# One fourth-degree polynomial in place of two refinement steps in every norm's inverse root, and the first half's mean taken ahead

## The chip, the cores and the metric

The kernel runs on one core of a Trainium2 chip. Its time is the device time of one execution in microseconds (us), as the median of three executions. The core has five engines with a queue of instructions each: TensorE (PE in the profile, its weight loads PEld), VectorE (DVE), ScalarE (ACT), GpSimd (POOL) and SyncE (SP), which issues most of the transfers. An engine takes its instructions strictly in the order of its queue, and waits on semaphores where data or buffers come from another engine.

## The reference

Two layers of an encoder trunk over 512 tokens of width 1024, in float32. Layer 0 mixes the tokens with a bidirectional gated recurrence (HGRN2, 8 heads), layer 1 with latent attention (MLA, 16 heads). Both then have the same MLP and a gated per-layer embedding, and everything is wrapped in RMS norms.

```
def rms_norm(x, gain):
    xf = x.astype(jnp.float32)
    y = xf * lax.rsqrt(jnp.mean(xf * xf, axis=-1, keepdims=True) + EPS)
    return (y * gain.astype(jnp.float32)).astype(x.dtype)

    for i in range(DEPTH):
        a = rms_norm(h, pre_mix_norm[i])
        ...                                   # m = hgrn2_mixer(a, ...) or mla_mixer(a, ...)
        h = h + rms_norm(m, post_mix_norm[i])
        f = squared_relu_mlp(rms_norm(h, pre_mlp_norm[i]), w_mlp_in[i], w_mlp_out[i])
        h = h + rms_norm(f, post_mlp_norm[i])
        e = p[i].astype(h.dtype) @ w_ple_proj[i]
        g = jax.nn.sigmoid(h @ w_ple_gate[i])
        h = h + rms_norm(g * e, ple_norm[i])
```

Inside the mixers, `hgrn2_mixer` norms every head's output, and `mla_mixer` norms the compressed query (width 384) and the compressed key and value (width 256). Only the `lax.rsqrt` of such norms is touched here.

## The kernel before

Every matrix product is made of three float32r passes over a high and a low part of both operands: for a weight, DMA brings `raw`, ACT casts it to `whi`, and DVE (at some places POOL) subtracts to get `wlo`; for activations the pairs are `ah`/`al`, `oh`/`ol`, `cqh`/`cql`, `Kh`/`Kl` and so on. A group of matmuls therefore waits for ACT and then for DVE. The products land in PSUM banks (`mm`, `sm`, `nm`), and a bank can be written again only when its reader, mostly an ACT or DVE instruction, is done.

A norm works on tokens as partitions: column t of a small tile belongs to token tile t (128 tokens). ACT squares a tile and sums along the row (`junk`, with the sum in `ssq`; one column for the first 512 elements of the row, one for the second). `Rms.mean` adds the two (`ssq`), scales and adds the epsilon (`sv`); `rsqrt` makes the inverse root (`sr`); then DVE updates the residual (`H<-F,sr,H`, called H below). `Rms.done` calls `mean` and `rsqrt`; `Rms.about` calls `mean` and only `guess`, a first approximation, for norms whose scale is put right later. `Norm.rs` uses `rsqrt` in the two norms of MLA (`nv` to `nr`, four columns), and `scan()` in each HGRN head (`oss` to `orr`, four columns). In the chains between the stages two token tiles go at a time (two columns); the last norm of the program takes one tile at a time (one column).

Before the change `rsqrt` is a shift and a multiply-add on the integer bits (`rq_i`, then `sr`), two scaled copies of the mean square (`rq_m`, `rq_n`), and two refinements: `rq_t` = y y m, then a product that sharpens it, then `sr`; and once more `rq_t` = y y m2 and `sr`. Each instruction but the two copies needs the one ahead of it.

What sets the order: a scheduler simulates the whole program and writes each engine's queue. Instructions issued through `V` it may move; in the stretches between the stages the program asks for program order on PE and on the norms' small operations (`VN`), among which it may still mix others. So the number and length of a few small instructions decide where casts, splits and residual updates stand around them. All go through one helper, so nearly every row of the profile shows line 147 (split helpers show 112), and rows are told apart by tile names.

The stretches of the prediction: the HGRN heads (50 to 305 us, the last head's recurrence about 260 to 305); the way from the layer-0 mixer to its MLP (about 335 to 355); the turn between the layers (about 735 to 760), where the gate's output gets its norm, H is updated and normed again (`r`), and PE transposes it for MLA's input product; MLA's start (780 to 813); and the end (from 1523).

Of the kernel before, what the change touches and what calls it, by code (L numbers as in the profile page):

```python
# [22 lines left out]
F32 = mybir.dt.float32  # L23
F32R = mybir.dt.float32r
I32 = mybir.dt.int32
AF = mybir.ActivationFunctionType
ALU = mybir.AluOpType
AX = mybir.AxisListType.X

P = 128  # L30
S = 512
D = 1024
NB = D // P
NT = S // P
# [127 lines left out]
def trunk(  # L162
# [7 lines left out]
    VN = Ordered(tc, nc.vector, V.mem)  # L170
# [7 lines left out]
    def T(pool, shape, tag, bufs=1, dt=F32):  # L178
        uid[0] += 1
        return pool.tile(list(shape), dt, tag=tag, bufs=bufs, name=f"{tag}_{uid[0]}")  # L180

    cst = ctx.enter_context(tc.tile_pool(name="cst", bufs=1))
# [189 lines left out]
    def linear_outer(keys, xs, pss=None, ws=None, ks=None):  # L372
# [6 lines left out]
                mm3(ps, cols(wh, n, P)[:, k], cols(wl, n, P)[:, k], xs[k][0], xs[k][1], k == 0, k == n - 1)  # L379
        return pss  # L380

    def rsqrt(v, y):


        n = v.shape[1]
        new = lambda tag, dt=F32: T(cst, [P, NT], tag, dt=dt, bufs=2)[:, :n]
        i, m, m2, t = new("rq_i", I32), new("rq_m"), new("rq_n"), new("rq_t")
        VN.tensor_scalar(i, v.bitcast(I32), 1, None, op0=ALU.logical_shift_right)
        VN.tensor_scalar(y.bitcast(I32), i, -1, 0x5F3759DF, op0=ALU.mult, op1=ALU.add)
        VN.tensor_scalar(m, v, 0.375 ** 0.5, None, op0=ALU.mult)  # L390
        VN.tensor_scalar(m2, v, -0.5, None, op0=ALU.mult)

        def times_squared(m):
            if n > 2:
                VN.tensor_mul(t, y, y)
                VN.tensor_mul(t, t, m)
            else:
                for c in range(n):
                    cs = slice(c, c + 1)
                    VN.scalar_tensor_tensor(t[:, cs], y[:, cs], m[:, cs], y[:, cs], op0=ALU.mult, op1=ALU.mult)  # L400


        times_squared(m)
        VN.scalar_tensor_tensor(t, t, -1.25 / 0.375 ** 0.5, t, op0=ALU.add, op1=ALU.mult)
        VN.scalar_tensor_tensor(y, t, 1.875, y, op0=ALU.add, op1=ALU.mult)
        times_squared(m2)
        VN.scalar_tensor_tensor(y, t, 1.5, y, op0=ALU.add, op1=ALU.mult)

    class Norm:

# [253 lines left out]
    for n in range(2):  # L664
        t = T(hp, [P, S], f"am{n}")
# [210 lines left out]
    for k in range(8):  # L876
        step({0: 2, 1: 2, 3: 1, 4: 1, 6: 1}.get(k, 0))
        if k < 7:
            if k % 2 == 0:
                w = W.next(("wo", 0, 0, 0, k // 2))  # L880
# [7 lines left out]
    half_of = lambda n: slice(n * S, n * S + S)  # L888
    espill = nc.dram_tensor("e_spill", (2, NT, P, D), F32).ap()

    def guess(v, y):

        i = T(cst, [P, NT], "gs_i", dt=I32, bufs=2)[:, : v.shape[1]]
        VN.tensor_scalar(i, v.bitcast(I32), 1, None, op0=ALU.logical_shift_right)
        VN.tensor_scalar(y.bitcast(I32), i, -1, 0x5F3759DF, op0=ALU.mult, op1=ALU.add)

    class Rms:


# [8 lines left out]
        def mean(self, ts):  # L908
            sl = slice(ts[0], ts[-1] + 1)
            v, u, w = self.v[:, sl], self.s[:, 0, sl], self.s[:, 1, sl]  # L910
            if self.halves:
                VN.tensor_add(u, u, w)
            if self.eps is None:
                VN.tensor_scalar(v, u, 1.0 / D, EPS, op0=ALU.mult, op1=ALU.add)
            else:
                VN.scalar_tensor_tensor(v, u, 1.0 / D, self.eps[:, sl], op0=ALU.mult, op1=ALU.add)
            return v, self.r[:, sl]

        def done(self, ts):
            rsqrt(*self.mean(ts))  # L920
            return self.r

        def about(self, ts):


            guess(*self.mean(ts))
            return self.r
# [339 lines left out]
    n, gate = mlp_to_gate(0, *mlp(0, act, pss, eps))  # L1267
# [91 lines left out]
    for k in range(2):  # L1359
        c = T(mp, [P, S], "P", 6)  # L1360
# [122 lines left out]
    for k in range(7):  # L1483
        if k % 2 == 0:
            w = W.next(("wo", 1, 1, 0, k // 2))
# [11 lines left out]
    n, gate = mlp_to_gate(1, *mlp(1, act, pss, eps))  # L1497


    for t in range(NT):  # L1500
        u = gate(t, V=VN, apart=True)
        r = n.done((t,))
        for c in range(2):
            cs = half_of(c)
# [56 lines left out]
```

## Time and profile before

| | before |
|---|---|
| median of 3 executions | 1533.91 us (1533.54 to 1535.32) |
| the profiled execution | 1534.51 us, its span 1532.8 us |
| PE busy | 1500.9 us, 98% of the span |
| DVE, ACT, POOL busy | 66%, 50%, 12% |
| mean granted TensorE clock | 0.996 of full |

Start with PE: it is busy nearly all the time, so the time can only shrink where PE waits, where its clock is low, or ahead of its first and behind its last matmul. The list of PE's waits says on which tile; the timeline of a wait then shows which instruction stood ahead in the releasing engine's queue. About 32 us of the span are not covered by PE, in many pieces that are mostly under 2 us.

### The profile page before, as it was taken

To read this page: it belongs to the slowest core of one execution; us is meant where nothing else is said; L and a number is where in the kernel's file an instruction comes from. 1 tells how busy PE (TensorE), PEld (TensorE's weight loads), DVE (VectorE), ACT (ScalarE), POOL (GpSimd) and SP (SyncE) were. 2 spreads that over 40 slices of the span, in tenths; PEclk is the share of its full clock that TensorE was granted. 3 is DMA by queue.
4 is the path that set the end of the run, shared out by engine and by line. 5 is a ranking of instruction groups with operands and counts; after the bars stand their busy time and mean duration, and the time that the engine had idled before them with its cause. 6 is when DMAs were issued, how large, how long until landed. Compare 5 with 4: busy or idle time off the path is not lost.

```text
span 1532.8 us, 19321 instructions
## 1 busy us (share of the span) xinstructions
PE 1500.9 (98%) x7403; PEld 1256.2 (82%) x7403; DVE 1013.1 (66%) x1816; ACT 772.8 (50%) x1327; POOL 191.1 (12%) x208
## 2 busy tenths in 40 slices
PE   9999999999999999999999999999999999999997
PEld 7888888889888787888887888888788887878886
DVE  5788568655575849456787784378464747677476
ACT  6655455256554454434645564466355645444332
POOL 5242132200000000000113331432000000000000
PEclk9999999999999999999999999999999999999999
DMA  6622332147050422323321111221452050604221
GB/s 190 184 83 56 83 83 84 41 128 255 29 192 28 152 68 83 110 70 123 119 88 30 42 56 52 63 75 37 174 197 83 26 194 1 220 1 137 73 92 55
DMA packets 110014, 147.86 MB, mean 96 GB/s; under 512 B 4845, under 2 KB 78178, under 8 KB 109666
## 3 DMA queue, kind: packets, MB, share of 16 engines
q1 hardware_dynamic: 109346, 145.58, 29.1%
q8 instruction: 58, 0.95, 0.3%
q10 hardware_dynamic: 576, 1.05, 0.2%
q14 instruction: 34, 0.28, 0.1%
HBM read 138.23 MB, written 8.39 MB: 96 GB/s over the span
## 4 chain that ended last, share of the span: by engine, by line
PE 88%; DVE 8%; ACT 3%; issue 1%; DMA 0%; POOL 0%; SPq 0%; DVEq 0%; ACTq 0%; POOLq 0%
PE mm L147 81%; PE sm L147 5%; DVE wlo L147 2%; PE nm L147 1%; DVE rope_d L147 1%; ACT whi L147 1%; DVE ol L147 1%; DVE r L268 1%; DVE F L147 1%; ACT junk L147 1%; DMA x<-in_x 0%; DVE al L147 0%; DVE rq_t L147 0%; DVE mx L147 0%; DVE rope_a L147 0%
## 5 line engine op out<-in xcount | busy, mean ns | idle before, releaser
L147 PE MATMUL mm<-ah,whi 128*128 128x512 f32 (+1 forms) x912 | 332.7, 370 | 2.3 <-ACT whi L147 1.0
L147 PE MATMUL mm<-ah,wlo 128*128 128x512 f32 (+1 forms) x912 | 329.6, 368 | 0.0
L147 PE MATMUL mm<-al,whi 128*128 128x512 f32 (+1 forms) x912 | 318.2, 368 | 0.0
L147 ACT CAST whi<-raw 128x1024 fp32r<-128x1024 f32 (+3 forms) x195 | 197.0, 1017 | 218.3 <-PE mm L147 184.2
L147 DVE TENSOR_TENSOR wlo<-raw,whi 128x1024 fp32r<-128x1024 f32 x165 | 207.4, 1266 | 141.3 <-ACT whi L147 139.7
L147 PEld LDWEIGHTS mm<-ah,whi 128*128 128x128 f32 x912 | 172.0, 189 | 31.5 <-ACT whi L147 2.6
L147 PEld LDWEIGHTS mm<-ah,wlo 128*128 128x128 f32 x912 | 172.0, 189 | 27.6
L147 PEld LDWEIGHTS mm<-al,whi 128*128 128x128 f32 x912 | 164.3, 189 | 27.1
L147 PE MATMUL mm<-wlo,oh 128*128 128x512 f32 x400 | 156.3, 391 | 4.0 <-DVE wlo L147 4.0
L147 DVE TENSOR_TENSOR wlo<-r,whi 128x1024 fp32r<-128x1024 f32 x84 | 102.0, 1221 | 80.9 <-ACT whi L147 80.9
L147 PE MATMUL mm<-whi,ol 128*128 128x512 f32 x400 | 154.8, 389 | 0.0
L147 PE MATMUL mm<-whi,oh 128*128 128x512 f32 x400 | 151.6, 392 | 0.7 <-DVE F L147 0.7
L147 ACT CAST whi<-r 128x1024 fp32r<-128x1024 f32 x84 | 87.3, 1051 | 90.9 <-PE mm L147 90.8
L147 PE MATMUL mm<-whi,al 128*128 128x512 f32 x304 | 119.1, 392 | 0.8 <-DVE al L147 0.8
L147 PE MATMUL mm<-whi,ah 128*128 128x512 f32 x304 | 119.3, 394 | 0.2 <-ACT ah L147 0.2
L147 PE MATMUL mm<-wlo,ah 128*128 128x512 f32 x304 | 118.7, 390 | 0.0
L112 POOL TENSOR_TENSOR wlo<-raw,whi 128x512 fp32r<-128x512 f32 (+2 forms) x40 | 38.2, 979 | 560.0 <-ACT whi L147 553.0
L147 PEld LDWEIGHTS mm<-wlo,oh 128*128 128x128 f32 x400 | 75.3, 188 | 21.0 <-DVE wlo L147 5.7
L147 PEld LDWEIGHTS mm<-whi,oh 128*128 128x128 f32 x400 | 75.2, 188 | 16.5 <-DVE F L147 1.1
L147 PEld LDWEIGHTS mm<-whi,ol 128*128 128x128 f32 x400 | 75.2, 188 | 15.6
L147 ACT CAST oh<-Z 128x512 fp32r<-128x512 f32 x84 | 51.5, 620 | 43.6 <-PE mm L147 42.6
L147 PEld LDWEIGHTS mm<-whi,al 128*128 128x128 f32 x304 | 57.1, 188 | 14.2 <-DVE al L147 2.5
(314 smaller groups left out, 2706.9 us busy)
## 6 DMA issues: line engine op xcount, KB each, us to landing
raw<-in_w_mlp_in SPq DMA_DIRECT2D x32, 1024.0 KB, 5.7
r<-in_w_mlp_out SPq DMA_DIRECT2D x24, 1024.0 KB, 8.6
raw<-in_hg_w_in SPq DMA_DIRECT2D x40, 512.0 KB, 5.3
raw<-in_w_mlp_out SPq DMA_DIRECT2D x8, 1024.0 KB, 5.0
raw<-in_w_ple_gate SPq DMA_DIRECT2D x8, 1024.0 KB, 5.7
raw<-in_mla_w_o SPq DMA_DIRECT2D x8, 1024.0 KB, 5.1
raw<-in_mla_w_uq SPq DMA_DIRECT2D x8, 576.0 KB, 4.0
raw<-in_hg_w_out SPq DMA_DIRECT2D x4, 1024.0 KB, 5.1
```

The costliest lines, as they stand in the source:

```text
L112: lo_eng.tensor_sub(dst(lo)[:, a], src(t)[:, a], f(dst(hi))[:, a])
L147: i = getattr(self.eng, name)(*args, **kw)
L268: nc.vector.tensor_sub(quad(t, *u), quad(t, *u), quad(t, *v))
```

## The change

`rsqrt` now takes the guess in one instruction (the integer bits, read as numbers, times -0.5 plus a constant), scales the mean square once (`rq_m`), forms z = y y m (`rq_z`), two quadratics in z that need only z (`rq_p`, `rq_q`), multiplies the first by y, and the two together. `guess`, used by `about` too, shrinks from two instructions to one. `mean` no longer adds the two half sums first: the first half's scaled sum with the epsilon is taken by one instruction that needs only the first column, and the second half is multiplied and added by another (`sv<-ssq,sv`).

```
     def rsqrt(v, y):
         n = v.shape[1]
-        VN.tensor_scalar(i, v.bitcast(I32), 1, None, op0=ALU.logical_shift_right)
-        VN.tensor_scalar(y.bitcast(I32), i, -1, 0x5F3759DF, op0=ALU.mult, op1=ALU.add)
-        VN.tensor_scalar(m, v, 0.375 ** 0.5, None, op0=ALU.mult)
-        VN.tensor_scalar(m2, v, -0.5, None, op0=ALU.mult)
...
-        times_squared(m)
-        VN.scalar_tensor_tensor(t, t, -1.25 / 0.375 ** 0.5, t, op0=ALU.add, op1=ALU.mult)
-        VN.scalar_tensor_tensor(y, t, 1.875, y, op0=ALU.add, op1=ALU.mult)
-        times_squared(m2)
-        VN.scalar_tensor_tensor(y, t, 1.5, y, op0=ALU.add, op1=ALU.mult)
+        guess(v, y)      # y bits = -0.5 * (v bits) + 0x5F3759DF, one tensor_scalar
+        VN.tensor_scalar(m, v, 0.7235449657159028, None, op0=ALU.mult)
...                       # z = y*y*m: two tensor_mul if n > 2, else one instruction per column
+        VN.scalar_tensor_tensor(p, z, -0.65371664, z, op0=ALU.add, op1=ALU.mult)
+        VN.scalar_tensor_tensor(q, z, -3.06928481, z, op0=ALU.add, op1=ALU.mult)
+        VN.scalar_tensor_tensor(p, p, 0.89352604, y, op0=ALU.add, op1=ALU.mult)
+        VN.scalar_tensor_tensor(y, q, 2.75651422, p, op0=ALU.add, op1=ALU.mult)
...
     def mean(self, ts):
-            if self.halves:
-                VN.tensor_add(u, u, w)
             if self.eps is None:
                 VN.tensor_scalar(v, u, 1.0 / D, EPS, op0=ALU.mult, op1=ALU.add)
...
+            if self.halves:
+                VN.scalar_tensor_tensor(v, w, 1.0 / D, v, op0=ALU.mult, op1=ALU.add)
```

VectorE's queue has 1592 rows where it had 1662; the other queues have the same instructions, some in another order. On VectorE, in the turn between the layers, the second norm (`sr_5545`, after it `sr_5511`) stands among the splits `al` of the first two token tiles. Before:

```order
L147 TENSOR_SCALAR sr_5545<-rq_i_6334 128x2
L147 TENSOR_SCALAR rq_m_6335<-sv_5544 128x2
L147 TENSOR_SCALAR rq_n_6336<-sv_5544 128x2
L147 SCALAR_TENSOR_TENSOR al_738_6076<-mm_6323,gains_82,ah_737_6075 128x256
L147 SCALAR_TENSOR_TENSOR rq_t_6337<-sr_5545,rq_m_6335 128x1 x2
L147 SCALAR_TENSOR_TENSOR rq_t_6337<-rq_t_6337 128x2
L147 SCALAR_TENSOR_TENSOR sr_5545<-rq_t_6337,sr_5545 128x2
L147 SCALAR_TENSOR_TENSOR rq_t_6337<-sr_5545,rq_n_6336 128x1 x2
L147 SCALAR_TENSOR_TENSOR sr_5545<-rq_t_6337,sr_5545 128x2
L147 SCALAR_TENSOR_TENSOR H_493<-F_2948,sr_5545,H_493 128x1024 x2
```

and after:

```order
L147 TENSOR_SCALAR sr_5511<-sv_5510 128x2
L147 TENSOR_SCALAR rq_m_6288<-sv_5510 128x2
L147 SCALAR_TENSOR_TENSOR al_730_6030<-sm_6250,gains_82,ah_729_6029 128x256
L147 SCALAR_TENSOR_TENSOR rq_z_6289<-sr_5511,rq_m_6288 128x1 x2
L147 SCALAR_TENSOR_TENSOR al_732_6032<-sm_6259,gains_82,ah_731_6031 128x256
L147 SCALAR_TENSOR_TENSOR al_734_6034<-mm_6268,gains_82,ah_733_6033 128x256
L147 SCALAR_TENSOR_TENSOR rq_p_6290<-rq_z_6289 128x2
L147 SCALAR_TENSOR_TENSOR rq_q_6291<-rq_z_6289 128x2
L147 SCALAR_TENSOR_TENSOR rq_p_6290<-rq_p_6290,sr_5511 128x2
L147 SCALAR_TENSOR_TENSOR sr_5511<-rq_q_6291,rq_p_6290 128x2
L147 SCALAR_TENSOR_TENSOR H_493<-F_2924,sr_5511,H_493 128x1024 x2
L147 SCALAR_TENSOR_TENSOR al_736_6036<-mm_6277,gains_82,ah_735_6035 128x256
```

The last of the eight `al` now stands behind H, the earlier ones further up, and fewer instructions depend on each other behind the seventh. On ACT in the same place, one of the weight casts that stood ahead of the first two `r<-H,sr` stands behind them, and the last `ah` of the eight behind the second pair of `Z<-mm`.

On VectorE at the start of MLA, the norm of the compressed key and value (`nr_6666`, after it `nr_6614`) ends among a weight split and the other norm's squares (`nacc`). Before:

```order
L147 SCALAR_TENSOR_TENSOR nr_6666<-rq_t_6729,nr_6666 128x4
L147 TENSOR_TENSOR rq_t_6729<-nr_6666 128x4
L112 TENSOR_TENSOR wlo_6847<-raw_6682,whi_6846 128x384
L147 TENSOR_TENSOR rq_t_6729<-rq_t_6729,rq_n_6728 128x4
L147 TENSOR_TENSOR nacc_6662<-nacc_6662,nsq_6815 128x512
L147 SCALAR_TENSOR_TENSOR nr_6666<-rq_t_6729,nr_6666 128x4
L147 SCALAR_TENSOR_TENSOR cql_829_6819<-mm_6766,gains_82,cqh_828_6818 128x512
L147 TENSOR_REDUCE nv_6664<-sm_6822 128x4
```

and after:

```order
L147 SCALAR_TENSOR_TENSOR rq_p_6676<-rq_p_6676,nr_6614 128x4
L147 SCALAR_TENSOR_TENSOR nr_6614<-rq_q_6677,rq_p_6676 128x4
L112 TENSOR_TENSOR wlo_6789<-raw_6630,whi_6788 128x384
L147 TENSOR_TENSOR nacc_6610<-nacc_6610,nsq_6760 128x512
L147 SCALAR_TENSOR_TENSOR cql_827_6764<-mm_6711,gains_82,cqh_826_6763 128x512
L147 SCALAR_TENSOR_TENSOR P_6737<-mm_6347,gains_82,rope_a_6688 128x512
L147 SCALAR_TENSOR_TENSOR P_6743<-mm_6348,gains_82,rope_a_6688 128x512
L147 TENSOR_REDUCE nv_6612<-sm_6767 128x4
```

The norm is complete ahead of the split and of `nacc`; PE's transposes of `nr` stand one matmul further up, ahead of those of `nacc`; and the two `P`, which need `nr`, stand ahead of the other norm's sum (`nv`), whose chain is spread over what follows.

On VectorE on the way from the layer-0 mixer to its MLP, the fourth weight split of the MLP's first group (`wlo_3283`, after it `wlo_3249`) stands near the second H update. Before:

```order
L147 SCALAR_TENSOR_TENSOR rq_t_3247<-rq_t_3247 128x2
L112 TENSOR_TENSOR wlo_3283<-raw_3163,whi_3282 128x1024
L147 SCALAR_TENSOR_TENSOR sr_2967<-rq_t_3247,sr_2967 128x2
L147 SCALAR_TENSOR_TENSOR al_429_2972<-sm_3206,gains_82,ah_428_2971 128x256
L147 SCALAR_TENSOR_TENSOR al_431_2974<-sm_3215,gains_82,ah_430_2973 128x256
L147 SCALAR_TENSOR_TENSOR al_433_2976<-mm_3224,gains_82,ah_432_2975 128x256
L147 SCALAR_TENSOR_TENSOR rq_t_3247<-sr_2967,rq_n_3246 128x1 x2
L147 SCALAR_TENSOR_TENSOR al_435_2978<-mm_3233,gains_82,ah_434_2977 128x256
L147 SCALAR_TENSOR_TENSOR sr_2967<-rq_t_3247,sr_2967 128x2
L147 SCALAR_TENSOR_TENSOR H_493<-F_2948,sr_2967,H_493 128x1024 x2
```

and after:

```order
L147 SCALAR_TENSOR_TENSOR rq_p_3217<-rq_p_3217,sr_2943 128x2
L147 SCALAR_TENSOR_TENSOR al_431_2950<-sm_3186,gains_82,ah_430_2949 128x256
L147 SCALAR_TENSOR_TENSOR al_433_2952<-mm_3195,gains_82,ah_432_2951 128x256
L147 SCALAR_TENSOR_TENSOR sr_2943<-rq_q_3218,rq_p_3217 128x2
L147 SCALAR_TENSOR_TENSOR H_493<-F_2924,sr_2943,H_493 128x1024 x2
L112 TENSOR_TENSOR wlo_3249<-raw_3134,whi_3248 128x1024
L147 SCALAR_TENSOR_TENSOR al_435_2954<-mm_3204,gains_82,ah_434_2953 128x256
```

The split and the last `al` went behind the two H. On ACT one of the last `e<-mm` went behind the first `junk<-H`.

In the HGRN heads PE's groups of a head's recurrence (`osq`, `D,E`, `v,As`) stand one to nine matmuls further up; in the last head, after the `am` copy that stood ahead of a `wlo` (272.54 us in the trace before), VectorE now takes `E<-E,oml,L` first, then the `e` copies, and the `wlo` behind those, and POOL takes `As` ahead of the two `D`. Near the layer-1 mixer's end some casts changed places with norms' instructions on ACT; the order of the MLPs' long stretches is as it was but for single `junk`.

## Rows read from the trace of the kernel before

**Rows 1.** The page's summary: span; busy us, share, instructions of an engine.
```profile
span 1532.8 us, 19321 instructions
PE 1500.9 (98%) x7403; PEld 1256.2 (82%) x7403; DVE 1013.1 (66%) x1816; ACT 772.8 (50%) x1327; POOL 191.1 (12%) x208
```

**Rows 2.** PE's waits: tile waited for, us in total, times, longest.
```profile
PE mm L147 <- ACT P L147: 2.2, 2, 1.9
...
PE sm L147 <- ACT r L147: 2.0, 3, 0.7
```

**Rows 3.** Timeline of the end, DVE: start, duration, instruction [idle before].
```profile
1526.02 0.16 DVE L147 TENSOR_TENSOR ssq<-ssq 128x1 f32<-128x1 f32 x1
1526.21 0.15 DVE L147 TENSOR_SCALAR sv<-ssq 128x1 f32<-128x1 f32 x1
...
1526.59 0.15 DVE L147 TENSOR_SCALAR sr<-rq_i 128x1 int32<-128x1 int32 x1
1526.66 0.14 DVE L147 TENSOR_SCALAR rq_m<-sv 128x1 f32<-128x1 f32 x1
...
1526.84 0.22 DVE L147 SCALAR_TENSOR_TENSOR rq_t<-sr,rq_m 128x1 f32<-128x1 f32 x1
1527.09 0.16 DVE L147 SCALAR_TENSOR_TENSOR rq_t<-rq_t 128x1 f32<-128x1 f32 x1
...
1527.93 0.75 DVE L147 SCALAR_TENSOR_TENSOR H<-F,sr,H 128x512 f32<-128x512 f32 x1
```

**Rows 4.** Timeline of the turn between the layers, PE and ACT.
```profile
737.98 1.04 ACT L147 CAST whi<-raw 128x1024 fp32r<-128x1024 f32 x1
738.92 2.19 ACT L147 ACTIVATE r<-H,sr 128x1024 f32<-128x1024 f32 x2
...
741.16 0.98 PE L147 MATMUL sm<-ident,r 128*128 128x128 f32 x7 [0.71 <-ACT r L147]
746.67 0.39 PE L147 MATMUL mm<-ah,whi 128*128 128x256 f32 x1 [0.44 <-DVE rq_n L147]
758.80 0.87 PE L147 MATMUL sm<-ident,r 128*128 128x128 f32 x6 [0.71 <-ACT r L147]
```

**Rows 5.** Timeline of the turn, the second norm on DVE and POOL beside it.
```profile
747.20 2.82 POOL L112 TENSOR_TENSOR wlo<-raw,whi 128x256 fp32r<-128x256 f32 x4 [445.42 <-ACT whi L147]
747.33 0.63 DVE L147 SCALAR_TENSOR_TENSOR rq_t<-rq_t 128x2 f32<-128x2 f32 x1
750.27 2.48 DVE L147 SCALAR_TENSOR_TENSOR H<-F,sr,H 128x1024 f32<-128x1024 f32 x2
```

**Rows 6.** Two windows: us, PE, PEld, DVE, ACT, POOL busy, granted clock, DMA share, GB/s.
```profile
281.80:285.20 3.40, 3.40 (x17) 3.30 (x16) 1.25 (x3) 1.01 (x8) 0.00 (x0) 0.50 0.00 0
800.60:804.10 3.50, 3.50 (x10) 2.71 (x9) 3.37 (x8) 1.23 (x2) 0.00 (x0) 0.51 0.51 169
```

**Rows 7.** Timeline of MLA's start, DVE and PE.
```profile
785.92 0.16 DVE L147 SCALAR_TENSOR_TENSOR nr<-rq_t,nr 128x4 f32<-128x4 f32 x1
787.92 1.40 DVE L147 SCALAR_TENSOR_TENSOR P<-mm,gains,rope_a 128x512 f32<-128x512 f32 x2
798.60 0.47 PE L147 MATMUL mm<-Kh,Qh 128*128 128x512 f32 x1 [1.07 <-ACT whi L147]
800.04 0.51 PE L147 MATMUL mm<-Kl,Qh 128*128 128x512 f32 x1 [0.97 <-DVE Kl L147]
```

**Rows 8.** Timeline of the last HGRN head, DVE and PE.
```profile
276.50 1.87 DVE L147 SCALAR_TENSOR_TENSOR E<-E,oml,L 128x512 f32<-128x512 f32 x1
279.85 0.55 PE L147 MATMUL nm<-ident,ke 128*128 128x128 f32 x3 [1.62 <-DVE state L147]
```

**Rows 9.** Timeline from the layer-0 mixer to its MLP, DVE and PE.
```profile
346.06 1.23 DVE L112 TENSOR_TENSOR wlo<-raw,whi 128x1024 fp32r<-128x1024 f32 x1
349.29 2.48 DVE L147 SCALAR_TENSOR_TENSOR H<-F,sr,H 128x1024 f32<-128x1024 f32 x2
350.18 0.28 PE L147 MATMUL mm<-ah,whi 128*128 128x256 f32 x1
```

More of the change, by code (lines that the diff above doesn't have):

```diff
@@ L380, in linear_outer, with guess @@
         return pss
+    def guess(v, y):
+        VN.tensor_scalar(y.bitcast(I32), v.bitcast(I32), -0.5, float(0x5F3759DF), op0=ALU.mult, op1=ALU.add)
     def rsqrt(v, y):
         n = v.shape[1]
-        new = lambda tag, dt=F32: T(cst, [P, NT], tag, dt=dt, bufs=2)[:, :n]
-        i, m, m2, t = new("rq_i", I32), new("rq_m"), new("rq_n"), new("rq_t")
-        VN.tensor_scalar(i, v.bitcast(I32), 1, None, op0=ALU.logical_shift_right)
-        VN.tensor_scalar(y.bitcast(I32), i, -1, 0x5F3759DF, op0=ALU.mult, op1=ALU.add)
-        VN.tensor_scalar(m, v, 0.375 ** 0.5, None, op0=ALU.mult)
-        VN.tensor_scalar(m2, v, -0.5, None, op0=ALU.mult)
[L393 to L400, printed above, removed]
-        times_squared(m)
-        VN.scalar_tensor_tensor(t, t, -1.25 / 0.375 ** 0.5, t, op0=ALU.add, op1=ALU.mult)
-        VN.scalar_tensor_tensor(y, t, 1.875, y, op0=ALU.add, op1=ALU.mult)
-        times_squared(m2)
-        VN.scalar_tensor_tensor(y, t, 1.5, y, op0=ALU.add, op1=ALU.mult)
+        m, z, p, q = (T(cst, [P, NT], tag, bufs=2)[:, :n] for tag in ("rq_m", "rq_z", "rq_p", "rq_q"))
+        guess(v, y)
+        VN.tensor_scalar(m, v, 0.7235449657159028, None, op0=ALU.mult)
+        if n > 2:
+            VN.tensor_mul(z, y, y)
+            VN.tensor_mul(z, z, m)
+        else:
+            for c in range(n):
+                cs = slice(c, c + 1)
+                VN.scalar_tensor_tensor(z[:, cs], y[:, cs], m[:, cs], y[:, cs], op0=ALU.mult, op1=ALU.mult)
+        VN.scalar_tensor_tensor(p, z, -0.65371664, z, op0=ALU.add, op1=ALU.mult)
+        VN.scalar_tensor_tensor(q, z, -3.06928481, z, op0=ALU.add, op1=ALU.mult)
+        VN.scalar_tensor_tensor(p, p, 0.89352604, y, op0=ALU.add, op1=ALU.mult)
+        VN.scalar_tensor_tensor(y, q, 2.75651422, p, op0=ALU.add, op1=ALU.mult)
     class Norm:
@@ L889, in trunk @@
     espill = nc.dram_tensor("e_spill", (2, NT, P, D), F32).ap()
[L891 to L895, printed above, removed]
     class Rms:
```

## The prediction

> **What bounds the kernel now.** I read the summary first: PE is busy 1500.9 us of a span of 1532.8 [rows 1], so at most 32 us can be had in all by anything that leaves the matmuls as they are, and PE's instructions are the same 6866 rows of its queue before and after. Then PE's waits, by the tile waited for [rows 2]: the list is short, the longest single wait of those shown is 1.9 us, and the small tiles of a norm hardly appear in it. The reader is to see that a shorter norm is not itself a time saved: it counts where the norm's result is what PE waits for, or where it lets a cast, a split or a residual update behind it start earlier. So I went through PE's waits in the timeline and asked of each which queue released it and what stands ahead there now. Last I read the granted clock in windows: it is at full speed but for two stretches at half speed, one in the last HGRN head and one at MLA's start, both behind waits of PE [rows 6].
>
> The profiled execution took 1534.51 us: its span and 1.7 us around it. That is 0.60 above the median of 1533.91. I sum against 1534.51 and take 0.60 off.
>
> **The end of the program.** Nothing covers the last norm, since PE has finished; the path is ssq, then the small instructions, then H and the last transfer. From the start of ssq at 1526.02 to the start of H at 1527.93 are 1.91 us [rows 3]. The starts tell two prices: an instruction that needs the one ahead of it starts 0.19 to 0.25 later (ssq to sv 0.19, rq_t to rq_t 0.25), one that doesn't starts 0.07 later (sr to rq_m). Now: the first half's sv is out of the way before; sv of the second half, guess 0.19 later, rq_m 0.07 beside it, rq_z 0.22 after the guess, rq_p 0.25 later, rq_q beside it, the product with y 0.20 after rq_p, the last product 0.20, H 0.20: 0.19 + 0.22 + 0.25 + 0.20 + 0.20 + 0.20 = 1.26. Gain 0.65. Two prices are not in the trace: the guess as one float operation on integer bits, and sv as an instruction with a third operand. From below they are the 0.15 of the tensor_scalar and from above the 0.22 of the slowest three-operand row [rows 3], so the gain lies between 0.5 and 0.75. I take **-0.63**.
>
> **The turn between the layers.** Three things.
> (a) PE's transposes of the first two tiles of r wait for r, the second time 0.71 with the resumption at 741.16; the three waits for r in this turn sum to 2.0 [rows 2, 4], so the first of this pair is about 0.6. ACT reaches r at 738.92, behind a cast of 1.04 whose start is 0.94 ahead of it [rows 4]. That cast now stands behind both r. The residual that r needs is done before, as ACT goes from the cast to r without a wait. So r comes 0.94 earlier, and PE, which needs both r before it can go on, resumes 0.9 earlier: -0.9. The cast's own product is the last of the four outputs of PE's next product, which starts several us later, so it has cover.
> (b) At 746.67 PE waits 0.44 [rows 4]. The record names rq_n, but PE reads nothing of it here; what frees its bank is the second Z<-mm on ACT. One ah now stands behind it instead of ahead: -0.4. What that ah feeds is the last of eight blocks of PE's product, which has as much cover.
> (c) At 758.80 PE waits 0.71 for r of the second pair [rows 4]. Its chain starts at H, 750.27 [rows 5]. One al and three dependent small instructions no longer stand ahead of H; and the refinement ran into POOL's four wlo from 747.20 on, where a product that takes 0.16 at the end of the program took 0.63 [rows 3, 5]. The chain now ends around 747.5 to 748, H starts some 2 us earlier, and the second norm behind it saves another 0.6: even with PE itself 1.3 earlier the wait goes, -0.7.
> Together **-2.0**. The cap is the sum of the waits, 2.0 + 0.44, with some refilling of PE around them: -3.0; the least is 0, if ACT loses at another cast what it gains here.
>
> A rule of the Trainium skill speaks against (c). The row shows the 0.63 product beside POOL's wlo [rows 5]. "SBUF — State Buffer", section "Who interferes with whom", says that a DVE instruction with two inputs in SBUF contends with a GpSimd instruction that reads SBUF, and that whichever issues later is blocked until the other is done. The row agrees: 0.63 is about one of the four POOL instructions. All four products of the new polynomial have two such inputs, so by the rule, if the chain is not through by 747.20, it is held for up to 4 x 0.47 = 1.9 us, H gains next to nothing, and the sum would lose the 0.7 of (c).
>
> **The start of MLA.** nr of the key and value norm is done at 785.92 + 0.16, behind a wlo and the nacc addition; P, which needs it, starts at 787.92 [rows 7]. Now both come behind nr, and three dependent instructions, 0.2 each [rows 3], are gone: nr is done some 1.5 us earlier. PE's transposes of nr move up by only one matmul, so P starts about 1 us earlier, and the other norm's chain, as much shorter, is spread over splits. PE waits 1.07 and 0.97 further down [rows 7]; the first ends when DVE frees the bank (rope_a<-mm,COS), the second with Kl, and both stand in this same DVE queue, which runs almost without a pause there (3.37 of 3.50 us in the window behind) [rows 6]. If DVE is 0.4 to 1.3 earlier there, so is PE: -1.0. The half-clock stretch behind it [rows 6] costs half of its 3.5 us, less what PE then waits for the next operand (stk): 1.4. I do not count on it going, and add -0.4 for the chance. **-1.4**, between -0.3 (only the small instructions' own time) and -3.5 (both waits and the stretch).
>
> **The last HGRN head.** PE waits 1.62 for state, and runs at half clock for 3.4 us a little later [rows 6, 8], which costs 1.7. The cause stands in DVE's queue: E takes 1.87 at 276.50 beside POOL, where instructions of the same size take 0.75 [rows 3, 8], and ke, which must precede state, waits for E and for the e copies behind a wlo. Now E and the e copies stand ahead of that wlo. The same work remains, so ke may be 1 to 2 us earlier or as late as now, if the contention with POOL falls elsewhere. **-0.9**, between +1.0 and -4.0. In the earlier heads PE hardly waits, and other matmuls stand between a head's norm and its transposes; no term.
>
> **From the layer-0 mixer to its MLP.** This is a loss. PE runs here without a wait and reaches the fourth group of the MLP's first block at 350.18 [rows 9]. The wlo that this group needs was at 346.06; it now stands behind both H. H starts at 349.29 now; the wlo (1.23) goes from ahead of it, an al too (256 columns, which I put at 0.45, between the 0.75 of 512 columns and the 0.16 of a small instruction [rows 3]), and some 0.3 of small instructions: H at 347.3. The two H take 2.48, the wlo 1.23: done at 351.0, against PE's need of the low part one matmul after 350.18, at about 350.3. **+0.65**, between 0 and +1.4. The e that went behind the first junk<-H is ready before that.
>
> **Elsewhere.** In layer 1's way to the MLP one wait on ACT may shrink by a cast's place; the gates lose a tenth here or there: 0, between -0.5 and +0.4. The MLPs are as they were.
>
> Sum: -0.63 - 2.0 - 1.4 - 0.9 + 0.65 = -4.3. 1534.51 - 4.3 - 0.60 = 1529.6; I forecast **1529.7 us**.
>
> **The rivals.**
> *The waits pass to others.* The tail's -0.63 and the cast's -0.9 at the turn are had, and the rest of PE's waits keep their length, since ACT or POOL release them a little later in their own order; layer 0 adds 0.65. -0.9: 1533.0, no change. For it: most of PE's waits are named for ACT or a bank, not for a norm. Against: at the turn the same queue order that shortens the norm moves the cast.
> *The clock stays up.* Both half-clock stretches follow waits that may now be shorter. If PE's waits ahead of them shrink to under 1 us, 1.7 and 1.4 come back on top, less the 0.4 counted: 1527.0. For it: both stretches come after waits of 1 to 1.6 us, which the change shortens [rows 7, 8]. Against: the longest wait of all, 1.9 for P [rows 2], has no such stretch behind it, so length alone doesn't tell.
> *Slower: the split behind H.* In layer 0 the wlo behind both H starts only when H does. If H starts as late as before (349.29), because the ah of ACT that its queue neighbours need come no earlier, the wlo ends at 353.0 and PE waits 2.7; a wait of that size may be followed by a half-clock stretch, 1.7 more. With the same delay the chains behind H lose what the turn gains: +4.4 - 0.6 gives 1537.7. It decides once H starts later than about 348.5, where PE's wait grows past the 1.62 that stands ahead of the half-clock stretch in the last head [rows 8]. Against it: ACT's order there has one cast fewer ahead of those ah.
>
> **How the numbers follow.** A change of 0.2%, 3.07 us, is about what can be told from none here; the bounds are 1530.84 and 1536.98. The forecast 0.50, its own range 1527.8 to 1531.5, with a tenth of all chance above 1530.84; the waits that pass on 0.28; the clock 0.12; the split 0.10, of which 0.08 beyond 1536.98. So faster 0.40 + 0.12 = 0.52, plus 0.03 of the second case; same 0.10 + 0.25 + 0.02 = 0.37; slower 0.08. The range for 8 in 10 runs from 1526.6, which holds nearly all of the clock's case, to 1533.8, above the second.
>
> **What would show it.** Right: H starts about 1.3 us behind ssq at the end; at the turn ACT goes to r without the cast and PE's two waits are one of under half a us, with none at the second r; P starts before PE's nacc product is reduced; PE shows a new wait of half a us for a wlo near 350. Wrong: PE's gaps at the turn and at MLA's start are as long as before with another releaser, or a stretch at half clock where there was none.

## The result, and the profile after

The changed kernel takes 1549.46 us (median of 4 executions, 1547.11 to 1549.87) where the one before, run beside it, takes 1534.49: a ratio of 1.0094 [1.0082, 1.0105]. The forecast was 1529.7 us; the change made the kernel 15 us slower. The page of the profiled execution (1549.87 us), against [rows 1]:

```profile
span 1548.1 us, 19250 instructions
PE 1515.2 (98%) x7403; PEld 1259.5 (81%) x7403; DVE 1000.0 (65%) x1738; ACT 771.9 (50%) x1327; POOL 191.4 (12%) x208
```

DVE has 13 us less to do, as the shorter polynomial says, and PE has the same 7403 instructions. But PE is busy 14.3 us longer. Waits are not the bulk of it then: the matmuls themselves take longer, or run at half clock.

To find where, I took the start of one and the same matmul (by its operands and its number among its kind) in the trace before and in another trace. The difference says how late the other kernel is at that point; the difference between two such points is what the stage between them lost (us; times are those of the kernel before; e1, e2 and e5 are experiments told below). Each column is one profiled execution, and the columns add up to the differences of the spans.

| stage, up to | forecast | after | e1: after, tiles back in place | e2: before, tiles shifted | e5: e1, order mended |
|---|---|---|---|---|---|
| first HGRN heads, 262.9 | 0 | +0.91 | +0.36 | +0.05 | +0.23 |
| last head and output product, 338.6 | -0.9 | +1.63 | -1.87 | -0.49 | -1.90 |
| way to layer 0's MLP, 363.7 | +0.65 | +0.48 | +0.83 | +0.26 | +0.43 |
| **layer 0's MLP and gate, 726.5** | 0 | **+4.11** | -0.01 | **+4.28** | +0.04 |
| turn between the layers, 767.3 | -2.0 | -1.16 | -1.20 | +0.02 | -1.18 |
| MLA's start, 826.9 | -1.4 | +1.02 | +1.94 | +0.06 | +0.81 |
| rest of MLA, 1128.4 | 0 | +0.06 | -0.10 | +0.07 | -0.50 |
| **way to layer 1's MLP, 1158.0** | 0 | **+4.75** | **+3.46** | +0.01 | -0.27 |
| **layer 1's MLP and gate, 1518.0** | 0 | **+4.07** | -0.03 | **+4.28** | 0.00 |
| the end | -0.63 | -0.52 | -0.28 | +0.17 | -0.51 |
| sum | -4.3 | +15.3 | +3.1 | +8.7 | -2.9 |

Three stages make 12.9 of the 15.3 us, and the forecast had 0 in each. How far can one execution be trusted? In the six experiments that keep the order of before (e2, e3, e8 to e11), the way to layer 1's MLP differs from before by 0.01 at most, and in the nine whose weights stand to `oh` and `ol` as before each MLP differs by 0.12 at most. The last head and MLA's start are less steady: in those six they come out between -1.5 and 0 and between +0.1 and +1.6, mostly by stretches at half clock that come and go (last section).

**The MLPs: a slower beat.** In the MLP PE hardly waits, in either kernel. Its timeline in a product of the MLP, first of the kernel before (start, duration, instruction):

```profile
519.94 0.39 PE L147 MATMUL mm<-whi,oh 128*128 128x512 f32 x1
520.17 0.39 PE L147 MATMUL mm<-wlo,oh 128*128 128x512 f32 x1
520.40 0.39 PE L147 MATMUL mm<-whi,ol 128*128 128x512 f32 x1
```

and the same kind of product in the kernel after, and some 50 us ahead of it another kind:

```profile
470.03 0.39 PE L147 MATMUL mm<-ah,wlo 128*128 128x512 f32 x1
470.26 0.39 PE L147 MATMUL mm<-ah,whi 128*128 128x512 f32 x1
470.49 0.39 PE L147 MATMUL mm<-al,whi 128*128 128x512 f32 x1
...
519.92 0.40 PE L147 MATMUL mm<-whi,ol 128*128 128x512 f32 x1
520.15 0.39 PE L147 MATMUL mm<-whi,oh 128*128 128x512 f32 x1
520.39 0.40 PE L147 MATMUL mm<-wlo,oh 128*128 128x512 f32 x1
```

The column to read is the first, not the second: matmuls overlap, so the duration hides the beat. `oh` and `ol` products start every 0.227 us before and every 0.233 after, while `ah` products keep 0.227 to the row. Over all 512-column matmuls the median from start to start goes from 227 ns to 233 or 234 for the 1200 with `oh` or `ol`, and to 232 to 235 for the 408 with `r` or `Z`; for the some 3100 whose operands are `ah` or `al` with `whi` or `wlo` it stays at 227 in both. 1608 times 6 ns are 9.6 us.

**The way to layer 1's MLP: a new wait and half clock behind it.** The timeline after, ACT, DVE and PE, and then a window (columns as in [rows 6]):

```profile
1144.14 1.05 ACT L147 CAST whi<-raw 128x1024 fp32r<-128x1024 f32 x1 [0.32 <-DMA raw<-in_w_mlp_in]
1144.20 2.48 DVE L147 SCALAR_TENSOR_TENSOR H<-F,sr,H 128x1024 f32<-128x1024 f32 x2
1145.10 0.83 ACT L147 ACTIVATE ah<-mm,gains 128x256 fp32r<-128x256 f32 x2
1146.59 0.87 DVE L147 SCALAR_TENSOR_TENSOR al<-mm,gains,ah 128x256 fp32r<-128x256 f32 x2
1147.22 0.55 PE L147 MATMUL mm<-ah,whi 128*128 128x256 f32 x1 [2.84 <-DVE al L147]
```

```profile
1147.00:1151.00 4.00, 3.78 (x18) 3.81 (x19) 2.34 (x8) 3.34 (x4) 0.00 (x0) 0.50 0.41 151
```

PE waits 2.84 us for a bank that the last two `al` read. They stand behind both H on DVE, since the shorter norm lets H go first, and the `ah` they need stand behind a weight cast on ACT. PE idled before the window and gets half its clock in it. In the kernel before, all `al` stood ahead of H and PE waited 0.94 here, for something else:

```profile
1137.55 0.38 PE L147 MATMUL mm<-ah,whi 128*128 128x256 f32 x1 [0.94 <-ACT e L147]
1138.84 0.48 DVE L147 SCALAR_TENSOR_TENSOR al<-mm,gains,ah 128x256 fp32r<-128x256 f32 x1 [0.15 <-ACT ah L147]
1139.24 2.47 DVE L147 SCALAR_TENSOR_TENSOR H<-F,sr,H 128x1024 f32<-128x1024 f32 x2
```

PE's waits after, for [rows 2]:

```profile
PE mm L147 <- DVE al L147: 3.3, 3, 2.8
PE mm L147 <- DVE rope_a L147: 2.5, 3, 1.4
PE mm L147 <- ACT P L147: 2.4, 2, 2.1
...
PE sm L147 <- ACT r L147: 0.4, 1, 0.4
```

Three waits for `r` of 2.0 us have become one of 0.4; longer ones stand elsewhere. The end on DVE, for [rows 3]:

```profile
1541.99 0.16 DVE L147 SCALAR_TENSOR_TENSOR sv<-ssq,sv 128x1 f32<-128x1 f32 x1
...
1543.27 0.75 DVE L147 SCALAR_TENSOR_TENSOR H<-F,sr,H 128x512 f32<-128x512 f32 x1
```

The turn, PE, ACT, DVE and POOL, for [rows 4, 5]:

```profile
745.11 2.18 ACT L147 ACTIVATE r<-H,sr 128x1024 f32<-128x1024 f32 x2
747.19 1.04 ACT L147 CAST whi<-raw 128x1024 fp32r<-128x1024 f32 x1
747.35 0.98 PE L147 MATMUL sm<-ident,r 128*128 128x128 f32 x7 [0.44 <-ACT r L147]
753.40 0.39 PE L147 MATMUL mm<-ah,whi 128*128 128x256 f32 x1 [0.71 <-ACT Z L147]
753.93 4.81 POOL L112 TENSOR_TENSOR wlo<-raw,whi 128x256 fp32r<-128x256 f32 x4 [453.16 <-ACT whi L147]
754.73 3.42 DVE L147 SCALAR_TENSOR_TENSOR H<-F,sr,H 128x1024 f32<-128x1024 f32 x2
```

MLA's start, DVE and PE, for [rows 7], and a window behind the wait for P:

```profile
794.24 0.68 DVE L147 TENSOR_REDUCE nv<-sm 128x4 f32<-128x512 f32 x1
799.71 1.29 DVE L147 TENSOR_SCALAR rq_m<-nv 128x4 f32<-128x4 f32 x1
801.01 2.79 DVE L147 TENSOR_TENSOR rope_d<-mm,SIN 32x512 f32<-32x512 f32 x4
804.67 0.47 PE L147 MATMUL mm<-Kh,Qh 128*128 128x512 f32 x1 [1.45 <-DVE rope_a L147]
806.59 0.50 PE L147 MATMUL mm<-Kl,Qh 128*128 128x512 f32 x1 [1.45 <-DVE Kl L147]
814.66 0.50 PE L147 MATMUL mm<-Kh,Qh 128*128 128x512 f32 x1 [2.05 <-ACT P L147]
```

```profile
814.60:818.60 4.00, 3.94 (x10) 3.04 (x11) 2.26 (x8) 3.84 (x11) 0.91 (x2) 0.57 0.00 0
```

The last head, DVE and PE, for [rows 8], and layer 0's way to its MLP, DVE, for [rows 9]:

```profile
274.53 1.89 DVE L147 SCALAR_TENSOR_TENSOR E<-E,oml,L 128x512 f32<-128x512 f32 x1 [0.85 <-ACT L L147]
276.56 2.33 DVE L147 TENSOR_TENSOR wlo<-raw,whi 128x1024 fp32r<-128x1024 f32 x1
281.46 0.55 PE L147 MATMUL nm<-ident,ke 128*128 128x128 f32 x3 [2.28 <-DVE state L147]
...
348.98 2.48 DVE L147 SCALAR_TENSOR_TENSOR H<-F,sr,H 128x1024 f32<-128x1024 f32 x2
351.38 1.22 DVE L112 TENSOR_TENSOR wlo<-raw,whi 128x1024 fp32r<-128x1024 f32 x1
```

### The profile page after: what moved, and what is told of

Same layout as the page of the kernel before. It is cut to its first block, busy times and chain, and to the rows that moved or that the text cites. A ratio compares the mean times of both kernels' runs of the same rounds, so it can differ in the third digit from the quotient of the medians.

```text
span 1548.1 us, 19250 instructions
## 1 busy us (share of the span) xinstructions
PE 1515.2 (98%) x7403; PEld 1259.5 (81%) x7403; DVE 1000.0 (65%) x1738; ACT 771.9 (50%) x1327; POOL 191.4 (12%) x208
## 4 chain that ended last, share of the span: by engine, by line
PE 89%; DVE 6%; ACT 3%; issue 1%; DMA 1%; POOL 0%; SPq 0%; DVEq 0%; ACTq 0%; POOLq 0%
PE mm L147 83%; PE sm L147 5%; DVE wlo L147 1%; PE nm L147 1%; ACT whi L147 1%; DVE rope_d L147 1%; DVE F L147 1%; DMA x<-in_x 1%; ACT junk L147 0%; DVE ol L147 0%; DVE al L147 0%; DVE r L268 0%; DVE mx L147 0%; POOL L L693 0%; ACT ah L147 0%
## 5 line engine op out<-in xcount | busy, mean ns | idle before, releaser
L147 DVE TENSOR_TENSOR F<-F,mm 128x512 f32<-128x512 f32 x68 | 46.3, 683 | 36.4 <-PE mm L147 36.0
```

The lines of the kernel that those rows point to most:

```text
L147: i = getattr(self.eng, name)(*args, **kw)
```

## The experiments

Why would a shorter norm slow a product that doesn't use it? What the two kernels do not share besides the order is where the tiles lie. The integer tile of `guess` (two buffers of 32 bytes per partition) is gone; the renamed small tiles beside it balance out. So every tile placed behind them from the left end of SBUF (`raw`, `whi`, `wlo`, `ah`, `al`) lies 64 bytes lower; those placed from the right end (`oh`, `ol`, `r`, `Z`, `pT` and MLA's) lie where they were. The slowed products have one operand from each side; `ah` and `whi` are both from the left. Theory A: the beat depends on the two operands' addresses. Its rivals: the change of order does it (theory B), or the clock or the chip (theory C).

In every comparison the kernel before is run on the same chip; its median is 1534.67 beside e1 to e4, 1535.38 beside e5 to e8 and 1535.39 beside e9 to e12. Its single executions spread from 1531.5 to 1537.2, so a kernel's worth is read from its interval, and the table of one execution each says only where the time went.

### e1 and e2: the 64 bytes put back, and taken away without the change

e1 is the kernel after with an unused tile; every queue's order is that of after. e2 is the kernel before with an unused tile that makes the left side lie 192 bytes higher, which is 64 lower by 256.

```
 # e1, in Rms.about of the kernel after
+            if not padded:
+                padded.append(T(cst, [P, 16], "gs_pad"))
 # e2, in Rms.about of the kernel before
+            if not padded:
+                padded.append(T(cst, [P, 48], "gs_pad"))
```

Expected of e1: 

> The changed kernel with an unused tile of 64 bytes per partition among the small ones, where the guess's integer tile was; every queue's order stays that of the changed kernel. Theory A (addresses): without that tile all weights and activations behind it lie 64 bytes lower, while the pools on the other side stay, and matmuls that read one operand from each side take 231 to 236 ns instead of 227; with the pad they take 227 again, and the time falls by 10 to 12 us, to 1537.5 to 1539.5. Theory B (order): the whole loss is in waits from the new order; the time stays at 1549 and the intervals at 233. Theory C (the clock or the chip): every 512-column matmul would be slower, those with both operands on one side too, and the pad changes nothing.

Expected of e2: 

> The kernel before with 192 unused bytes per partition at the same place, so that its weights stand to the other side's pools as in the changed kernel, counted modulo 256 bytes; its order stays. Theory A: wlo and whi with oh, ol, r, Z and pT at 231 to 236 ns, 10 to 12 us slower than before, 1544.5 to 1546.5, and no new wait. Theories B and C: 1534.5.

Measured: e1 1537.75, ratio 1.0023 [1.0013, 1.0032]; e2 1544.98, ratio 1.0068 [1.0049, 1.0087]. PE's timeline of e1, then of e2:

```profile
520.65 0.39 PE L147 MATMUL mm<-wlo,oh 128*128 128x512 f32 x1
520.88 0.39 PE L147 MATMUL mm<-whi,ol 128*128 128x512 f32 x1
```

```profile
520.92 0.39 PE L147 MATMUL mm<-whi,oh 128*128 128x512 f32 x1
521.15 0.40 PE L147 MATMUL mm<-wlo,oh 128*128 128x512 f32 x1
```

The beat follows the bytes in both directions: 0.227 with the change and the pad, 0.233 without the change. By the medians the 64 bytes are worth 12 us of the 15 in the changed kernel (after against e1) and 10 us in the kernel before (e2), where the norm has no part in them. The table shows it by stage: the two MLPs lose 4.1 each in after, nothing in e1, 4.28 each in e2. In the profiled executions after loses another 4 us against e1, mostly in the last head and its output product (3.5) and on the way to layer 1's MLP (1.3). Some 1.0 of the 3.5 is the beat again: 192 products with `oh` and `ol` stand there, and that stage is -0.49 in e2 and -1.5 in e9 and e11, which differ in the bytes alone. The rest is a longer wait and half clock; that the addresses cause these is not shown. The remaining 3 us of e1 are order: its way to layer 1's MLP alone loses 3.46.

### e3, e9, e10 and e11: which property of the addresses

All are the kernel before with a pad: e3 and e9 on the left ([P, 32] and [P, 64], 128 and 256 bytes), e10 on the right, e11 on both sides (192 left, 64 right; what lies on the right gets lower).

```
 # e10 and e11
-    T(ctx.enter_context(right("pad")), [P, 8], "pad")
+    T(ctx.enter_context(right("pad")), [P, 24], "pad")
```

Expected of e3: 

> The kernel before with 128 unused bytes there. If only whether the two operands stand alike modulo 128 matters, 1534.5 and 227 ns; if modulo 256, the matmuls with oh, ol, r, Z and pT rise to 229 to 232 ns (1720 of them, some 3.5 ns each), about 6 us slower, 1540.5, while the products of cqh and ckh with weights, 232 ns before, fall to 227 and give back about 1 us. Theories B and C: 1534.5.

Expected of e9: 

> The kernel before, order unchanged, with 256 unused bytes among the small tiles. Theory A (a relation modulo 256 bytes between the two operands): back to 227 ns and 1534.5 to 1535.5, although more was added than in the slow versions with 128 and 192. Rival G (any shift of the weights from their old place costs, or memory used costs): 231 to 236 ns and 1543 to 1546.

Expected of e10: 

> The kernel before, order unchanged, with the first tile of the other side's pools 64 bytes larger: oh, ol, r, Z, pT lie 64 bytes lower and the weights stay. Theory A: as slow as moving the weights, 231 to 236 ns for products of weights with oh, ol, r, Z and pT, 1543.5 to 1546. Rival H (only the moving weights' own address counts): 227 ns and 1534.5 to 1535.5.

Expected of e11: 

> The kernel before, order unchanged, with both changes: 192 bytes on the weights' side and 64 on the other, so that both sides stand as in the first case of before modulo 256, at other addresses. Theory A: 227 ns, 1534.5 to 1535.5. Rival H, or a rule on absolute addresses of either side: 231 to 236 ns and 1543 to 1546 as each of the two alone.

Measured: e3 1542.87, ratio 1.0056 [1.0038, 1.0073]; e9 1533.99, 0.9992 [0.9983, 1.0001]; e10 1537.83, 1.0017 [1.0007, 1.0027]; e11 1534.90, 0.9999 [0.9990, 1.0009]. The medians from start to start, in ns, against the address of the moving operand minus that of the stationary one, modulo 256 (the moving operand is the first named after the arrow; the addresses are those of the built kernels):

| kernel | left, right moved by | `whi,oh`: difference, ns | `whi,r`: ns | `cqh,whi`: difference, ns | `ah,whi`: ns |
|---|---|---|---|---|---|
| before | 0, 0 | 0, 227 | 227 | 128, 232 | 227 |
| after | -64, 0 | 192, 234 | 235 | 192, 235 | 227 |
| e1 | 0, 0 | 0, 227 | 227 | 128, 232 | 227 |
| e2 | +192, 0 | 192, 234 | 235 | 192, 235.5 | 227 |
| e3 | +128, 0 | 128, 232 | 232 | 0, 228.5 | 227 |
| e9 | +256, 0 | 0, 227 | 227 | 128, 233 | 227 |
| e10 | 0, -64 | 64, 229 | 229 | 64, 232 | 227 |
| e11 | +192, -64 | 0, 227 | 227 | 128, 232 | 227 |

Only the difference counts, not the address: e11 moves both sides and keeps the beat. 256 bytes are a full turn (e9). At a difference of 0 the product is fast; at 64, 128 and 192 `whi,oh` is slower, in this order. Over all 14 traces, and all products outside MLA, the median is 227 ns at 0, 229 at 64, 232 at 128 and 233 at 192. At 64 the products differ among themselves, from 227.5 (`whi,Z`) to 232 (`wlo,r`). Whether the matmul's own weights count, or those of the next one, is not separated: neighbours mostly stand at the same difference. Two misses in size: e3 came out slower than expected, at eight tenths of e2's loss, and e10 was expected to be as slow as e2, on the wrong idea that plus and minus 64 are alike; it lost 2.4 us. The theory's core stood, its symmetry fell.

### e6 and e7: which half of the change moves the order

e6 is the kernel after with the pad and the old mean; e7 is the kernel before with the mean taken ahead alone (its small tiles, and so its addresses, are those of before).

```
 # e6, in Rms.mean of the kernel after
+            if self.halves:
+                VN.tensor_add(u, u, w)
...
-                VN.scalar_tensor_tensor(v, w, 1.0 / D, v, op0=ALU.mult, op1=ALU.add)
 # e7 is the reverse edit in the kernel before
```

Expected of e6: 

> The changed kernel's guess and polynomial with the mean as it was before, weights at their old addresses (64-byte pad). Theory E (the shorter polynomial moves the two last al behind H): a wait of 2.5 to 3 us for al near 1140 as in the padded changed kernel, 1537 to 1538.5. Theory F (the mean taken ahead does it): no such wait, 1533 to 1534.5.

Expected of e7: 

> The kernel before with only the first half's mean taken ahead; all tiles keep their addresses. Theory E: 0.2 us less at the end, waits as before but for the place of one al between the two H in layer 1, 1533.5 to 1535. Theory F: the 2.8 us wait near 1140 appears, 1537 to 1538.5.

Measured: e6 1538.03, ratio 1.0019 [1.0010, 1.0029]; e7 1535.15, 0.9999 [0.9989, 1.0008]. The way to layer 1's MLP in e6, DVE and PE:

```profile
1136.36 2.48 DVE L147 SCALAR_TENSOR_TENSOR H<-F,sr,H 128x1024 f32<-128x1024 f32 x2
1138.75 0.87 DVE L147 SCALAR_TENSOR_TENSOR al<-mm,gains,ah 128x256 fp32r<-128x256 f32 x2
1139.38 0.55 PE L147 MATMUL mm<-ah,whi 128*128 128x256 f32 x1 [2.90 <-DVE al L147]
```

The guess and the polynomial alone put the two `al` behind H and make the wait. The mean taken ahead, alone, is worth nothing that can be told.

### e4, e5 and e12: the order mended

e4 is e1 with H made to follow the last `al` of its turn on DVE. e5 adds that the casts of the next weights' first piece follow the last `ah` on ACT, and 128 unused bytes among MLA's tiles, which bring `cqh,whi` to a difference of 0 (`cqh`, `ckh`, `Vh` and their like move, `PTh` stays). e12 is e5 without those 128 bytes.

```
 # e4, in add_residual; last is the last al that split() issued
+            j = VN.scalar_tensor_tensor(H[:, t], F[:, t], r[:, t : t + 1], H[:, t], op0=ALU.mult, op1=ALU.add)
+            tc.add_manual_dep(j.ins, last.ins.name, ...)
 # e5 besides, at the casts whose key is ("w1", ..., 0, ...); after is the last ah
+                c = self.hi.copy(dst(hi), src(t))
+                self.hi.tc.add_manual_dep(c.ins, self.after.ins.name, ...)
...
+            mla_padded.append(T(mp, [P, 32], "mla_pad"))
```

Expected of e4: 

> The padded changed kernel, with each second residual update held behind the last split al of the turn ahead of it (a dependence on the same engine). Theory A with order: the wait of 2.84 us for al near 1147 in the changed kernel and the half-clock stretch behind it (3.4 us at half speed, 1.7 lost) go, so 4 to 4.5 us under the padded one, 1533.5 to 1535. Theory D (that wait is made up for elsewhere): less than 1 us under the padded one.

Expected of e5: 

> The changed kernel with the 64-byte pad, each second residual update behind the turn's last al, the casts of the MLP's first weights behind the turn's last ah on ACT, and 128 unused bytes in MLA's pool between Vl and the small tiles ahead of PTh, so that cqh, cql, ckh, ckl, Vh and Vl stand to the weights and to PTh, PTl alike modulo 256 bytes. Theory A (addresses) with order: the wait near 1138 falls from 1.8 to under 0.8 and the half-clock stretch behind it goes (1.0 + 1.7), and 216 products of cqh, cql with weights, 96 or more of ckh, ckl and 192 of PTh, PTl with Vh, Vl take 227 instead of 232 (some 2 us): 1531 to 1533. If the rule of 256 bytes does not hold for these, 1533 to 1534. Theory D (waits are made up for elsewhere): 1535.5, as the padded one with al first.

Expected of e12: 

> The changed kernel with the 64-byte pad, the residual updates behind the last al and the casts behind the last ah, without the bytes in MLA's pool. If those bytes gave what their faster products suggest (1 to 2 us), 1534.2 to 1535.2 against 1533.2 with them; if the rest is due to order and the clock alone, 1533.2.

Measured: e4 1535.84, ratio 1.0005 [0.9995, 1.0015]; e5 1533.22, 0.9986 [0.9977, 0.9996]; e12 1533.64, 0.9993 [0.9983, 1.0002]. The way to layer 1's MLP in e4, ACT, DVE and PE:

```profile
1136.45 1.04 ACT L147 CAST whi<-raw 128x1024 fp32r<-128x1024 f32 x1
1137.90 0.88 DVE L147 SCALAR_TENSOR_TENSOR al<-mm,gains,ah 128x256 fp32r<-128x256 f32 x2 [1.12 <-ACT ah L147]
1138.53 0.51 PE L147 MATMUL mm<-ah,whi 128*128 128x256 f32 x1 [1.66 <-DVE al L147]
```

and in e5, with a window:

```profile
1135.01 0.48 DVE L151 SCALAR_TENSOR_TENSOR al<-mm,gains,ah 128x256 fp32r<-128x256 f32 x1 [0.31 <-ACT ah L151]
1135.22 1.06 ACT L151 CAST whi<-raw 128x1024 fp32r<-128x1024 f32 x1
1135.64 0.36 PE L151 MATMUL mm<-ah,whi 128*128 128x256 f32 x1 [0.47 <-DVE rq_p L151]
```

```profile
1135.00:1139.00 4.00, 3.53 (x30) 3.39 (x29) 3.49 (x6) 2.52 (x5) 0.00 (x0) 1.00 1.04 317
```

e4 fell short: DVE is free for the `al`, but now waits itself for an `ah` behind the cast, so half of the wait stays. It stood in two queues. In e5 ACT and DVE both have the operands of PE's next group first, the wait is 0.47, and the granted clock stays at 1.00. By the table the stage is then 0.27 better than before, and the whole profile 2.9 us shorter. But 1.9 of that stand in the last head, where e12, with the same order, gains 0.5. By its median e5 is the fastest version, by 2.2 us or 0.14%, with an interval that just leaves out no gain. e12's does not; whether MLA's 128 bytes are worth the 0.4 between them stays open.

### e8: MLA's operands alone

e8 is the kernel before with e5's 128 bytes among MLA's tiles.

```
+            mla_padded.append(T(mp, [P, 32], "mla_pad"))
```

Expected: 

> The kernel before, order unchanged, with the 128 unused bytes in MLA's pool alone. Theory A with the rule of 256 bytes: cqh, cql, ckh, ckl with weights and PTh, PTl with Vh, Vl go from 230 to 234 ns to 227 to 228; 500 products at some 4.5 ns give 2 us, 1532.5; Kh with Qh stays as it was, since both move together. If other reasons slow these products (weight loads, other traffic on the memory), no change: 1534.5.

Measured: 1535.09, ratio 0.9999 [0.9990, 1.0008]. `cqh,whi` goes from 232 to 229 ns and `cql,whi` from 231 to 227, as the rule says. The gain expected did not come. The 312 products of `cqh`, `cql`, `ckh` and `ckl` give 0.9 us by their medians, less than the interval can tell, and `PTh,Vh`, for which the same rule gave 0 now, stayed at 234. Nor is it alone: in MLA's attention `Kh,Qh` and `Kl,Qh` stand at 0 in every kernel, with medians of 231 to 235. Their intervals spread to above 300 ns. The fastest quarter of them does follow the rule: the lower quartile of `PTl,Vh` is 232 or 233 in the twelve traces where its difference is 128, and 227 in e5 and e8, where it is 0; that of `Kh,Qh` is 227 or 228 throughout. What sets the rest was not found.

## Why the prediction was wrong

**The step that failed is "The MLPs are as they were".** It was argued from the order of the queues, and the order is as it was. It left out that the diff removes a tile, and with it moves every tile placed behind it. Nearly half of PE's time is spent in the MLPs and gates (723 of 1533 us, by the stages above); 6 ns more on four in ten of their matmuls cost 8.2 us, more than all the terms of the sum together. The bounds had no place for it: the range left out anything beyond what PE's waits could give or take. The trace of before held a sign: the products of `cqh` with weights start every 232 ns there, those of `ah` every 227.

**"In layer 1's way to MLP one wait on ACT may shrink: 0" failed too**, by 4.75 in after and 3.46 in e1, of which a longer stretch at half clock in after is part. The rival named slower had the right mechanism, a split behind both H with half clock behind the wait, priced at 4.4; it had it in layer 0, where PE's spare work covered it (in e1 a wait of 0.55 appears, in after none). By these rows what decides is whether PE reaches the group before the pair of H ends. In layer 0 the answer was worked out from rows. In layer 1 the same swap stood in the order and was not asked.

The other steps:

- The end: 1.28 us from the second half's sv to H; the working said 1.26. Counted to the start of H the end gained 0.52 of 0.63, in after, e1 and e5 alike (what follows H differs by up to 0.25 from trace to trace), since the first half's sv stands right ahead of the second's and pushes it by a tenth. Right.
- The turn: ACT goes to `r` without the cast, one wait of 0.44 for `r` is left, and that at 758.80 is gone, as forecast. But -1.2 in place of -2.0: (b) failed. The wait for `Z`'s bank did not shrink, it grew from 0.44 to 0.71. (c) held although the chain was not through when POOL began: its last product (0.69 at 754.00) and H meet POOL's `wlo`, H with 3.42 for 2.48 before, and POOL's four take 4.81 for 2.82. The rule of the Trainium skill weighed there ("SBUF — State Buffer", "Who interferes with whom") agrees with these rows: the contention did not go, it met other instructions; but H had the room.
- MLA's start: +1.0 and +1.9 for a forecast -1.4. P comes 1.0 earlier than PE's own lateness would have it (787.92 to 792.91, with PE 6.0 late), as worked out. The step that failed is the next one, that `rope_a` follows it. DVE runs without a pause there, and P went ahead of the reduction of `nv` (0.7), which so stands between P and `rope_d` now; and `rq_m`, 0.16 elsewhere, takes 1.29 beside POOL's `wlo`. P to `rope_d` is 7.02 before and 8.10 after, and PE's two waits grow by 0.86 in all. This is steady: they sum to 2.90 in all six kernels with the changed chain (after, e1, e4, e5, e6, e12), and to 2.0 to 2.2 in the eight with the old order or nearly so. Moving work ahead in a full queue moves other work behind. The rest of the stage is clock. After has no half clock behind these two waits and has it behind the wait for P (granted 0.57, some 1.7 us); e1 has both. Kernels with the old order have the one, the other, both or none, so the forecast's -0.4 for the chance can't be judged from one trace.
- The last head: -0.9, bounds +1.0 and -4.0. The way forecast is right and the size is smaller: PE's wait for `state` is 1.2 in five of the six kernels with the changed chain (e1, e4, e5, e6, e12), and 1.6 in all eight others, so 0.4 are gained. The table's -1.9 in e1 and e5 is that and luck: no half clock follows there, while it follows the same wait in e4 and e12 (-0.4 and -0.5). After loses 1.6: its wait is 2.28, half clock follows as in before, and the output product has the slower beat. The `wlo` at 276.56 takes 2.33 beside POOL's two `D` there. In e1 it takes 1.21, and POOL's two `D` 3.94 in place of 3.50: in both traces the two engines start within 0.04 us of each other, and in after the split waits, in e1 POOL does. Which instruction meets POOL was not foreseen, and why the same order meets it differently in after was not settled.
- Layer 0's way: +0.65, measured +0.48 in after and +0.83 in e1. The term is right in e1, where PE waits 0.55 at the fourth group, though for `al`. In after PE shows no wait of 0.2 or more here, and half of its 0.48 is the slower beat (e2 loses 0.26 by placement alone): there the number is right by luck.

## What to carry to other kernels

Before an edit that adds or removes a tile is priced by its instructions, compare the built addresses of every matmul's two operands before and after; here 64 bytes of scratch cost 10 to 12 us and all that the edit itself did to the order 3. Read the beat of a pipelined engine from its starts: the mean duration of `whi,oh` went from 392 to 397 ns, the busy share stayed at 98%, and neither shows it. Before a stretch at half clock that appears or goes is put down to an edit, look whether it does so among traces of one order. And where a norm gets shorter, ask at each place what its residual update now runs ahead of, and mend both queues that feed the late operand, as e4 against e5 shows.

## What the runs showed of the hardware that was not expected

- Outside MLA, a 512-column float32r matmul starts every 227, 229, 232 or 233 ns, by the median, as moving minus stationary address, modulo 256 bytes, is 0, 64, 128 or 192 (14 traces). The Trainium skill ("SBUF — State Buffer", section "Who interferes with whom") counts the moving operand's reads and the weights' as independent ports; by that no placement would cost anything. The intervals differ, so the measurement stands. It was shown for placement in steps of 64 bytes only, and in MLA's attention only the fastest quarter of the intervals follows, not the medians.
- A 128x4 `rq_m` of 0.16 us took 1.29 beside POOL, in all six kernels with the changed chain. It has one input in SBUF; the same section of the Trainium skill names tensor_scalar among those that can still meet POOL, and the row agrees.
- Half clock (1.2 in place of 2.4 GHz) came behind a wait of 2.84 us in after and of 1.66 in e4 (granted 0.57 from 1138.5 to 1142.5). Behind other waits it comes and goes among executions of one order. In the last head, behind a wait of 1.6: yes in before, e7 and e8, no in e2, e3, e9, e10 and e11; behind 1.2: yes in e4 and e12, no in e1, e5 and e6. In MLA's start, with a pair of waits of 1.0 to 1.2 and one of 1.9 to 2.05 for P: behind the pair in before and e2, behind P in e3, e9 and e10, behind both in e8 and e11, behind neither in e7. Each such stretch costs some 1.7 us. The length of a wait alone does not tell, and what does was not tried.
